# Strassen weights in quarter layout, fifth and sixth product exchanged, chores of the first mixer tied to landed exchanges

## The chip, the core and the metric

The kernel runs on one core of a Trainium2 chip. Its time is the device time of one execution in microseconds (us). The kernel before took 1366.08 us (median of 3 runs, 1362.96 to 1366.48).

A core has five engines that run side by side, each with its own stream of instructions in a fixed order: TensorE (PE) multiplies matrices into PSUM banks, VectorE (DVE) and ScalarE (ACT) work on tiles, GpSimd (POOL) does a few products and issues some of the DMAs, SyncE (SP) issues most of the DMAs. An engine waits at an instruction until the semaphores of what it needs are set; all behind it on that engine waits too.

## The reference

Two layers over 512 tokens of width 1024. Layer 0 mixes tokens by eight heads of bidirectional retention and eight heads of 8 x 16 neighbourhood attention, layer 1 by a Mamba-2 scan. Behind each mixer stands a GeGLU channel mixer ("ffn") of width 2816 with a width-3 convolution in front of the activation.

```python
u = rms_norm(x, g) @ w_up                 # 1024 -> 2 x 2816, gate and value
u = depthwise_conv_centered(u, cw, cb)    # width 3 along the tokens
h = gelu(u[..., :2816]) * u[..., 2816:]
x = x + rms_norm(h @ w_down, g_post)
```

In layer 0 the queries and keys of the retention heads are turned by rotary angles first: every head's two halves change places, one is multiplied by the sine, the other by the cosine.

## The kernel before

**A product in three.** Everything is float32, and every matrix is split into a rounded high part and the rest, so that one product becomes three passes: high by high, low by high, high by low (`mm3`, L124 to L126). A weight tile of 128x1024 (512 KB) is loaded by SP into a staging buffer (`wst`, three of them), cast by ACT to its high part (L115), and DVE subtracts that to give the low part (L116). Both parts go to one of four places of `ring`, from where PE takes them.

**Stages.** In the trace the first mixer lies at about 60 to 250 us, its ffn at 270 to 600, the second mixer at 600 to 1015, the second ffn at 1015 to the end.

**The up projection of the ffn.** Of its 22 blocks of 128 gate and 128 value features, twelve are done in six pairs per ffn (`UP` = 6, 8, 10, 14, 16, 18) by Strassen's scheme: seven products instead of eight (`up_strassen`). A pair's weights are a 2x2 matrix of quarters: gate or value, first or second 512 inputs, each for two blocks of features. Each product has 24 matmuls of 256 columns. The weights of the products are, in order: q11 (the A11 product); q12 + q22 (S3); that plus q11, in the tile `gain` (S2); that plus q21 (A22); q11 with a fourth quarter added to it by an accumulating DMA from POOL (L473; R1); q21 (A12); q22 (S4). In memory a quarter lies as two runs of 2 KB in each partition's row of two blocks, and is gathered by an access pattern (`places`).

The products accumulate in three PSUM banks: A11, S2, R1, S4 in bank a (`mm`), S3 and A22 in bank b (`pu`), A12 in bank d (`pu`). Between two products of one bank ACT or DVE reads the intermediate result from it (L497, L500 by ACT; L458 by DVE), and the next product of that bank waits for that reading.

**Order.** A scheduler puts the instructions of every engine in order by the code's order, by priority (`high_priority(60)` draws a step ahead) and by when operands should be ready. The order is fixed when the kernel is built.

**Chores.** While all this runs, POOL prepares the down projection: `sums` (L284) makes 704 KB copies and accumulations of quarters of `w_down` in DRAM. A chore is tied behind the last matmul issued so far (`E.product`). One is issued at each `c` of the strings `PAIRS` in the first mixer, which say in which order the steps of each pair of heads go; in a Strassen pair one is issued behind the second and one behind the fifth product.

**Rotary exchange.** In the first mixer, for queries and for keys of a pair of heads, ACT copies the projected tile to `ra` (L734), four SP DMAs fetch its 32-row bands exchanged into `rb` (L736), POOL multiplies `rb` by the sine (L737), DVE multiplies `ra` by the cosine (L738) and adds the two (L739), and ACT casts the sum to `rq` or `rk` (L720, L722).

**Neighbourhood attention.** The exponentials `e` are scaled by DVE (L856), transposed by PE to `pt` (L864), copied to `w` by ACT or DVE in turn (L866, in `nb_weights`), and multiplied with the values into `y` (L874).

Of the kernel before, what the change touches and what calls it, by code (L numbers as in the profile page):

```python
# [8 lines left out]
F32 = mybir.dt.float32  # L9
# [4 lines left out]
ALU = mybir.AluOpType  # L14
# [3 lines left out]
P = 128  # L18
# [5 lines left out]
FFN = 2816  # L24
# [7 lines left out]
class Env:  # L32
# [33 lines left out]

        self.xh, self.xl = (self.res.tile([P, KD, S], R32, name=n, tag=n) for n in ("xh", "xl"))

    def chore(self, n=1):

        for _ in range(min(n, len(self.chores))):
            self.together([self.chores.pop(0)()], [self.product])

    def wload(self, src, behind=None):

# [319 lines left out]
UP = (6, 8, 10, 14, 16, 18)  # L395
# [41 lines left out]
def up_strassen(E, pool, w_up, f, X, G, V, held):  # L437

    nc, tc = E.nc, E.tc
    low, high = slice(0, HW), slice(HW, S)

    def places(st, s, h):
        return (st.rearrange("p (f c) -> p f c", f=2),
                w_up[s, f:f + 2, :, h * 512:h * 512 + 512].rearrange("f p c -> p f c"))

    def load(pool, name, s, h, tag=None):
        st = pool.tile([P, 1024], F32, name=name, tag=tag or name)
        nc.sync.dma_start(*places(st, s, h))  # L450
        return st

    def parts(st, i):
        hi, lo = E.weight(SKEW if i else 0)
        E.split(hi, lo, st)
        return hi, lo

    add = lambda o, x, y: nc.vector.tensor_tensor(o, x, y, op=ALU.add)  # L458
    q = {}

    def weights(i):
        with tc.high_priority(60):
            if i == 0:
                q[11] = load(E.wst, "wst", 0, 0)
                return parts(q[11], i)
            if i == 1:
                q[12], q[22] = load(E.wst, "wst", 1, 0), load(pool, "wu", 1, 1, f"e{UP.index(f) % 2}")
                add(q[12], q[12], q[22])
                return parts(q[12], i)
            if i == 2:  # L470
                q[0] = E.gain.tile([P, D], F32, name="gain")
                add(q[0], q[11], q[12])
                nc.gpsimd.dma_start(*places(q[11], 1, 0), accum_op=ALU.add, max_dma_last_dim=4096)  # L473
                return parts(q[0], i)
            if i == 3:
                q[21] = load(E.gain, "gain", 0, 1)
                add(q[0], q[0], q[21])
                return parts(q[0], i)
            return parts(q[{4: 11, 5: 21, 6: 22}[i]], i)

    a = E.mm.tile([P, S], F32, name="mm")
    b, d = (E.px.tile([P, S], F32, name="pu", tag="px") for _ in range(2))
    order = ("A11", a), ("S3", b), ("S2", a), ("A22", b), ("R1", a), ("A12", d), ("S4", a)
    for i, (n, bank) in enumerate(order):
        hi, lo = weights(i)
        more = i in (2, 3, 4, 6)
        r = bank.rearrange("p (j c) -> p j c", j=2)
        for j in range(2):
            for k in range(4):
                c = slice(j * 512 + k * P, j * 512 + k * P + P)  # L490
                E.mm3(r[:, j], hi[:, c], lo[:, c], X[n][0][:, k], X[n][1][:, k], not more and j + k == 0, k == 3, more or j > 0)
        if i in (3, 5):
            o = G[:, :, low if i == 3 else high]
            add(o, r, o)
        elif i == 4:
            t = E.tmp.tile([P, 2, HW], F32, name="w5", tag="tmp")
            nc.scalar.copy(t, r)  # L497
            add(V[:, :, low], t, V[:, :, low])
        else:
            nc.scalar.copy({0: G[:, :, high], 1: V[:, :, low], 2: G[:, :, low], 6: V[:, :, high]}[i], r)  # L500
        if i in (1, 4):
            E.chore()
        if i in (3, 5) and held:
            held.pop(0)()


# [79 lines left out]
def log1p_exp_neg(E, alloc, z):  # L586
# [25 lines left out]


PAIRS = (
# [4 lines left out]
)  # L619


def mixer0(E, w0, w_v, w_fm, tabs, dist_d, logit, gn, bias, w_out, g_post_row, done):
# [3 lines left out]
    nc, tc = E.nc, E.tc  # L626
    with ExitStack() as ctx:
        pool = lambda name, bufs: ctx.enter_context(tc.tile_pool(name=name, bufs=bufs))
        one, two, sd, bp = pool("m0", 1), pool("m0b", 2), pool("m0s", 7), pool("m0n", 2)

        rot = one.tile([P, 2, S], F32, name="rot")
# [30 lines left out]
        for s in range(2):  # L662
            ps = [E.mm.tile([P, 512], F32, name="mm") for _ in range(NT)]
            for u in range(4):
                w = w0.pop(0) if w0 else E.wunit(w_v[s, u])
                for t in range(NT):
                    tt = slice(t * P, (t + 1) * P)
                    for i in range(2):
                        k = 2 * u + i
# [56 lines left out]
        def project(p, o, nm):  # L726
            i = ("rk", "rq", "rg", "nq", "nk").index(nm)
            w = E.wunit(w_fm[i, p])
            ps = E.mm.tile([P, S], F32, name="mm")
            E.proj_fm(ps, w)  # L730
            if i < 2:
                a = E.tmp.tile([P, S], F32, name="ra", tag="tmp")
                b = E.tmp.tile([P, S], F32, name="rb", tag="tmp")
                nc.scalar.activation(a, ps, AF.Copy, scale=1.0 if i else 0.125)  # L734
                for j in range(4):
                    nc.sync.dma_start(b[32 * j:32 * j + 32], a[32 * (j ^ 1):32 * (j ^ 1) + 32])  # L736
                nc.gpsimd.tensor_tensor(b, b, rot[:, 1], op=ALU.mult)  # L737
                nc.vector.tensor_tensor(a, a, rot[:, 0], op=ALU.mult)  # L738
                nc.vector.tensor_tensor(a, a, b, op=ALU.add)  # L739
                o[nm] = (twice if i else stack)(nm, a)  # L740
                o[nm + "a"] = a
            elif i == 2:
                o[nm] = two.tile([P, S], F32, name=nm)
                nc.scalar.activation(o[nm], ps, AF.Silu)
            elif i == 3:
                o[nm] = stack(nm, ps.rearrange("p (r b c) -> p b r c", r=8, b=4))
            else:
                o[nm] = twice(nm, ps, 0.125)
# [110 lines left out]
        def nb_weights(p, o, i):  # L859

            pt = E.px.tile([P, 2, 2, P], F32, name="pt", tag="px")
            for j in range(2):
                for k in range(2):
                    nc.tensor.transpose(pt[:, j, k], o["e", i][:, j, k * P:(k + 1) * P], E.ident)  # L864
            o["w", i] = sd.tile([P, 2, 2, P], F32, name="w", tag="sd")
            (nc.scalar.copy if i % 2 else nc.vector.tensor_copy)(o["w", i], pt)  # L866

        def nb_values(p, o):
            y = E.px.tile([P, 4, P], F32, name="y", tag="px")
# [487 lines left out]
def _cols(w):  # L1357

    f = w.shape[1]
    return w.reshape(KD, P, f // P, P).transpose(2, 1, 0, 3).reshape(f // P, P, 1024)  # L1360
# [42 lines left out]
def _layouts(np, i):  # L1403
    a = {"x": i["x"][0]}
# [32 lines left out]

    for l in range(2):
        w = i["ffn_w_up"][l]
        a[f"f{l}_up"] = np.stack([_cols(w[:, s * FFN:(s + 1) * FFN]) for s in range(2)])  # L1440
        cw = np.concatenate([i["ffn_conv_w"][l], i["ffn_conv_b"][l][None]])
        a[f"f{l}_cw"] = cw.reshape(4, 2, NF, P).transpose(3, 1, 2, 0)
        a[f"f{l}_down"] = _quarters(np, i["ffn_w_down"][l])
# [29 lines left out]
```

## Time and profile before

| | |
|---|---|
| median of 3 runs | 1366.08 us (1362.96 to 1366.48) |
| profiled execution | 1359.76 us, its span 1358.0 us |
| granted clock of TensorE, mean | 0.999 |
| PE busy | 1328.2 us (98% of the span) |
| DVE busy | 1106.3 us (81%) |
| ACT busy | 829.8 us (61%) |
| POOL busy | 127.4 us (9%) |
| bytes moved | 236.23 MB, of it 52.43 MB by POOL's queue |

The page of the profile comes from one execution. Its span runs from the first instruction to the last; 1.76 us of the execution lie around it. PE counts as busy from the start of a matmul to its modelled end, so that matmuls that overlap in the pipeline hide small waits: what PE waits for is better read from the list of waits, or from the starts of its matmuls.

### The profile page before, as it was taken

The page shows a single profiled execution, that of the slowest core. Times are in us where ns is not written, and L with a number is a line of the kernel's source. Part 1 is how long each engine was busy: PE and PEld are TensorE (multiplying, and loading weights), DVE is VectorE, ACT ScalarE, POOL GpSimd, SP SyncE. Part 2 cuts the span into 40 slices and gives each one's busy share as a digit, 9 for nine tenths or more (in the row PEclk, how much of TensorE's full clock was granted, in tenths as well). Part 3 has the DMA queues.
Part 4 walks back from the last instruction along what each step waited for, and adds up shares of the span by engine and source line. Part 5 has one row for each costly group of instructions (what it writes and reads, how often), then busy time and mean ns, then how long its engine had stood idle before and what let it go on. Part 6 is the DMA issues. An engine that isn't in the chain of part 4 may idle for free.

```text
span 1358.0 us, 20142 instructions
## 1 busy us (share of the span) xinstructions
PE 1328.2 (98%) x7640; PEld 1134.6 (84%) x7640; DVE 1106.3 (81%) x1536; ACT 829.8 (61%) x1337; POOL 127.4 (9%) x142
## 2 busy tenths in 40 slices
PE   7999999999999999999999999999999999999997
PEld 6877877898999988888778788787879899998886
DVE  7368778696699998797878876798789789989886
ACT  5356667453564666564878878477545467566663
POOL 1011111111110000010000110011011111110001
PEclk9999999999999999999999999999999999999999
DMA  8454446339894545663565475285545788884554
GB/s 300 143 185 152 159 154 211 105 120 225 177 211 116 143 132 189 198 203 130 139 183 190 129 250 184 92 246 165 183 132 180 191 196 192 192 201 140 190 181 148
DMA packets 78785, 236.23 MB, mean 174 GB/s; under 512 B 8544, under 2 KB 9312, under 8 KB 78176
## 3 DMA queue, kind: packets, MB, share of 16 engines
q1 hardware_dynamic: 60368, 167.30, 37.5%
q0 software_dynamic: 10432, 52.43, 17.1%
q10 hardware_dynamic: 7888, 15.21, 4.2%
q8 instruction: 60, 0.98, 0.3%
q14 instruction: 37, 0.30, 0.1%
HBM read 227.30 MB, written 51.64 MB: 205 GB/s over the span
## 4 chain that ended last, share of the span: by engine, by line
PE 72%; DVE 9%; DMA 7%; ACT 6%; issue 4%; POOL 1%; SPq 0%; DVEq 0%; POOLq 0%; ACTq 0%
PE mm L124 19%; PE mm L126 19%; PE mm L125 19%; DMA pb<-pd 2%; DVE ring L116 2%; PE pu L125 2%; DMA wst<-in_f_up 2%; PE pu L126 2%; PE pu L124 2%; ACT pb L1115 1%; PE st L1085 1%; PE pi L1136 1%; DMA rb<-ra 1%; ACT ring L115 1%; PE pt L181 1%
## 5 line engine op out<-in xcount | busy, mean ns | idle before, releaser
L124 PE MATMUL mm<-xh,ring 128*128 128x512 f32 (+2 forms) x928 | 341.4, 368 | 1.0 <-ACT z L1055 0.4
L126 PE MATMUL mm<-xl,ring 128*128 128x512 f32 (+2 forms) x928 | 340.6, 368 | 1.1 <-DVE mean L939 0.6
L125 PE MATMUL mm<-xh,ring 128*128 128x512 f32 (+2 forms) x928 | 340.3, 367 | 1.0 <-DVE ring L116 1.0
L116 DVE TENSOR_TENSOR ring<-wst,ring 128x1024 fp32r<-128x1024 f32 (+1 forms) x220 | 266.9, 1219 | 64.8 <-ACT ring L115 64.5
L115 ACT CAST ring<-wst 128x1024 fp32r<-128x1024 f32 (+1 forms) x220 | 226.2, 1034 | 123.8 <-PE mm L125 62.4
L124 PEld LDWEIGHTS mm<-xh,ring 128*128 128x128 f32 (+1 forms) x928 | 174.4, 188 | 31.2 <-issue 2.6
L126 PEld LDWEIGHTS mm<-xl,ring 128*128 128x128 f32 (+1 forms) x928 | 174.1, 188 | 30.7 <-issue 1.3
L125 PEld LDWEIGHTS mm<-xh,ring 128*128 128x128 f32 (+1 forms) x928 | 174.4, 188 | 29.2 <-DVE ring L116 1.4
L1115 ACT ACTIVATE pb<-pb,tok 128x128 f32<-128x128 f32 x256 | 80.7, 393 | 11.5 <-DMA pb<-pd 10.3
L124 PE MATMUL mm<-xc,ring 128*128 128x256 f32 x288 | 80.1, 278 | 1.7 <-ACT G L500 1.7
L125 PE MATMUL mm<-xc,ring 128*128 128x256 f32 x288 | 79.9, 277 | 0.0
L126 PE MATMUL mm<-xc,ring 128*128 128x256 f32 x288 | 79.8, 277 | 0.0
L124 PE MATMUL mm<-ring,big 128*128 128x512 f32 x164 | 64.0, 390 | 0.0
L126 PE MATMUL mm<-ring,big 128*128 128x512 f32 x164 | 63.8, 389 | 0.0
L125 PE MATMUL mm<-ring,big 128*128 128x512 f32 x164 | 63.8, 389 | 0.0
L518 ACT ACTIVATE cv<-mm,cwt 128x512 f32<-128x512 f32 x40 | 31.1, 777 | 52.1 <-PE mm L126 52.1
L284 POOL DMA_DIRECT2D ts<-in_f_down x48 | 32.0, 674 | 285.5 <-PE mm L126 206.1
L124 PEld LDWEIGHTS mm<-xc,ring 128*128 128x128 f32 x288 | 54.1, 188 | 2.1 <-ACT G L500 2.1
L126 PEld LDWEIGHTS mm<-xc,ring 128*128 128x128 f32 x288 | 54.1, 188 | 0.0
L125 PEld LDWEIGHTS mm<-xc,ring 128*128 128x128 f32 x288 | 54.0, 188 | 0.0
L125 PE MATMUL pu<-xh,ring 128*128 128x256 f32 x192 | 53.5, 279 | 0.2 <-DVE ring L116 0.2
L124 PE MATMUL pu<-xh,ring 128*128 128x256 f32 x192 | 53.3, 277 | 0.0
(360 smaller groups left out, 3064.2 us busy)
## 6 DMA issues: line engine op xcount, KB each, us to landing
ts<-in_f_down POOLq DMA_DIRECT2D x48, 704.0 KB, 6.2
wst<-in_f_up SPq DMA_DIRECT2D x64, 512.0 KB
wst<-in_c_fm SPq DMA_DIRECT2D x40, 512.0 KB
wst<-ts SPq DMA_DIRECT2D x32, 512.0 KB
pb<-pd ACTq DMA_DIRECT2D x29, 512.0 KB
wst<-in_f_down SPq DMA_DIRECT2D x24, 512.0 KB
ts<-ts POOLq DMA_DIRECT2D x16, 704.0 KB, 8.8
wst<-in_ab_fm SPq DMA_DIRECT2D x20, 512.0 KB
```

The source lines that it names most:

```text
L115: first = self.nc.scalar.copy(hi, src)
L116: second = self.nc.vector.tensor_tensor(lo, src, hi.bitcast(F32), op=ALU.subtract)
L124: mm(out, lh, rh, start=first, stop=False)
L125: mm(out, ll, rh, start=False, stop=False)
L126: self.product = mm(out, lh, rl, start=False, stop=last)
L181: last = nc.tensor.transpose(pt[:, j], xs[:, j * P:(j + 1) * P], self.ident)
L284: out.append(lambda i=i, src=src, j=j, c=c, kw=kw: gp.dma_start(part(ts, i, c), part(src, j, c), **kw))
L518: nc.scalar.activation(o, ps, AF.Identity, scale=w(1), bias=w(3))
L1085: nc.tensor.matmul(ps, o["bt"][:, c], xs, start=True, stop=True)
L1115: nc.scalar.activation(pb[:, dr, c], pb[:, dr, c], AF.Identity, scale=1.0 - 2 * dr, bias=tok[:, 0, c, dr * H + h:dr * H + h + 1])
L1136: nc.tensor.matmul(pi[:, c - 1 + dr], o["st"][dr, i][:, q * P:(q + 1) * P], o["t"][1][:, c * C:(c + 1) * C], start=True, stop=True)
```

## The change

1. The host lays the weights of the twelve Strassen blocks out by quarters, and a quarter's load is one contiguous run of 4 KB per partition instead of two of 2 KB. This holds for the three loads on SP per pair, for the fourth into `gain`, and for POOL's accumulating DMA.
2. The products go in the order 0, 1, 2, 3, 5, 4, 6: A12 comes before R1. The second chore stays behind the fifth product, which is now A12; the two places at which a pending tail of the blocks before is issued stay behind the fourth and the sixth.
3. The staging buffer of q12 is allocated ahead of that of q11.
4. In the first mixer the chore behind a pair's `v2` (in the strings: `v2 c`) is left out, and one is issued behind POOL's sine multiplication of the pair's second exchange instead, tied to that multiplication.
5. The copies to `w` in `nb_weights` get priority 60.

```diff
-    def chore(self, n=1):
+    def chore(self, n=1, behind=None):
...
-            self.together([self.chores.pop(0)()], [self.product])
+            self.together([self.chores.pop(0)()], [behind or self.product])
...
-    def places(st, s, h):
-        return (st.rearrange("p (f c) -> p f c", f=2),
-                w_up[s, f:f + 2, :, h * 512:h * 512 + 512].rearrange("f p c -> p f c"))
-
-    def load(pool, name, s, h, tag=None):
-        st = pool.tile([P, 1024], F32, name=name, tag=tag or name)
-        nc.sync.dma_start(*places(st, s, h))
+    def load(pool, name, s, h, tag=None, st=None):
+        st = pool.tile([P, 1024], F32, name=name, tag=tag or name) if st is None else st
+        nc.sync.dma_start(st, w_up[s, f + h])
...
             if i == 0:
+                q[12] = E.wst.tile([P, 1024], F32, name="wst")
                 q[11] = load(E.wst, "wst", 0, 0)
...
-                q[12], q[22] = load(E.wst, "wst", 1, 0), load(pool, "wu", 1, 1, f"e{UP.index(f) % 2}")
+                load(E.wst, "wst", 1, 0, st=q[12])
+                q[22] = load(pool, "wu", 1, 1, f"e{UP.index(f) % 2}")
...
-                nc.gpsimd.dma_start(*places(q[11], 1, 0), accum_op=ALU.add, max_dma_last_dim=4096)
+                nc.gpsimd.dma_start(q[11], w_up[1, f], accum_op=ALU.add, max_dma_last_dim=4096)
...
-    for i, (n, bank) in enumerate(order):
+    for i in (0, 1, 2, 3, 5, 4, 6):
+        n, bank = order[i]
...
-        if i in (1, 4):
+        if i in (1, 5):
             E.chore()
-        if i in (3, 5) and held:
+        if i in (3, 4) and held:
...
-    "nq rq rk nk rg c k d s0 m a0 a1 v0 c w0 s2 a2 a3 v2 c w1 w2 n w3 o",
+    "nq rq rk nk rg c k d s0 m a0 a1 v0 c w0 s2 a2 a3 v2 w1 w2 n w3 o",
...
-                nc.gpsimd.tensor_tensor(b, b, rot[:, 1], op=ALU.mult)
+                turned = nc.gpsimd.tensor_tensor(b, b, rot[:, 1], op=ALU.mult)
+                if "ra" in o:
+                    E.chore(behind=turned)
+                o["ra"] = a
...
-            (nc.scalar.copy if i % 2 else nc.vector.tensor_copy)(o["w", i], pt)
+            with tc.high_priority(60):
+                (nc.scalar.copy if i % 2 else nc.vector.tensor_copy)(o["w", i], pt)
```

The scheduler turns this into other orders on the engines. Three places follow, each as the order stands before and as it stands now. Lines of the changed kernel are one to three higher or a few lower than those of the kernel before.

DVE, between the second pair and the third of the first triple of the first ffn. Here `gain_3380` holds the summed weights of the second pair's A22 product, `wst_3578` before and `wst_3549` after are the third pair's q12, `gain_3611` its S2 weights, `wst_3318` before and `wst_3319` after the second pair's q11 (for R1), `gain_3410` the second pair's q21 (for A12). A row in which `ring` comes from a weight tile makes the low part. Before:

```order
L458 TENSOR_TENSOR gain_3380<-gain_3380,gain_3410 128x1024
L520 SCALAR_TENSOR_TENSOR cv0_3440<-G_3102,cwt_2558,cv0_3440 128x511
L519 SCALAR_TENSOR_TENSOR cv1_3445<-V_3103,cwn_2560,cv1_3445 128x511
L116 TENSOR_TENSOR ring_69<-gain_3380,ring_69 128x1024
L520 SCALAR_TENSOR_TENSOR cv1_3445<-V_3103,cwn_2560,cv1_3445 128x511
L458 TENSOR_TENSOR wst_3578<-wst_3578,wu_3580 128x1024
L116 TENSOR_TENSOR ring_69<-wst_3318,ring_69 128x1024
```

And now:

```order
L454 TENSOR_TENSOR gain_3380<-gain_3380,gain_3410 128x1024
L519 SCALAR_TENSOR_TENSOR cv0_3440<-G_3102,cwt_2558,cv0_3440 128x511
L518 SCALAR_TENSOR_TENSOR cv1_3445<-V_3103,cwn_2560,cv1_3445 128x511
L454 TENSOR_TENSOR wst_3549<-wst_3549,wu_3580 128x1024
L116 TENSOR_TENSOR ring_69<-gain_3380,ring_69 128x1024
L116 TENSOR_TENSOR ring_69<-gain_3410,ring_69 128x1024
L519 SCALAR_TENSOR_TENSOR cv1_3445<-V_3103,cwn_2560,cv1_3445 128x511
L454 TENSOR_TENSOR gain_3611<-wst_3550,wst_3549 128x1024
```

The sum for the third pair (`wst` from `wst` and `wu`), which needs a load, has moved ahead of the low part of the second pair's A22 weights.

PE, at the end of the first pair. `mm_3104` is bank a of that pair, `pu_3106` its bank d, `mm_3315` bank a of the second pair; `xc` marks combined operands (here R1, then S4), `xh` and `xl` the plain ones. Before, the end of A12's 24 matmuls, which followed on R1's last, and S4's first:

```order
L124 MATMUL pu_3106<-xh_61,ring_69 128x256
L125 MATMUL pu_3106<-xh_61,ring_69 128x256
L126 MATMUL pu_3106<-xl_62,ring_69 128x256
L124 MATMUL mm_3104<-xc_2878,ring_69 128x256
L125 MATMUL mm_3104<-xc_2878,ring_69 128x256
```

And now, R1's last, six of the next pair's A11, and S4's first:

```order
L126 MATMUL mm_3104<-xc_2878,ring_69 128x256
L124 MATMUL mm_3315<-xh_61,ring_69 128x256
L125 MATMUL mm_3315<-xh_61,ring_69 128x256
L126 MATMUL mm_3315<-xl_62,ring_69 128x256
L124 MATMUL mm_3315<-xh_61,ring_69 128x256
L125 MATMUL mm_3315<-xh_61,ring_69 128x256
L126 MATMUL mm_3315<-xl_62,ring_69 128x256
L124 MATMUL mm_3104<-xc_2878,ring_69 128x256
```

Between R1 and S4, which share bank a, there were 24 matmuls and there are 6 now. This is so behind the first two pairs of each triple; behind the third the scheduler puts four matmuls of 512 columns of a plain block between them.

ACT, in the first mixer between the first and the second pair of heads. `rq0` and `rq1` are the turned queries, `w_938` the copy of transposed exponentials, `rs` and `cat4` belong to the normalisation and the output. Before:

```order
L820 ACTIVATE sq_923<-y_839 128x512
L720 ACTIVATE rq0_997<-ra_987 64x512
L722 ACTIVATE rq0_997<-ra_987 64x512
L866 COPY w_938<-pt_933 128x512
L825 ACT_TABLE_LOAD
L825 ACTIVATE rs_927<-rs_927 128x512
```

And now:

```order
L822 ACTIVATE sq_923<-y_840 128x512
L719 ACTIVATE rq0_997<-ra_987 64x512
L869 COPY w_938<-pt_933 128x512
L827 ACT_TABLE_LOAD
L827 ACTIVATE rs_927<-rs_927 128x512
L879 COPY cat4_553<-y_940 128x4x8x16
L721 ACTIVATE rq0_997<-ra_987 64x512
```

The copy to `w_938` still stands behind the first cast of the turned queries, but the second cast has moved behind it and behind the normalisation.

More of the change, by code (lines that the diff above doesn't have):

```diff
@@ L1439, in _layouts @@
         w = i["ffn_w_up"][l]
-        a[f"f{l}_up"] = np.stack([_cols(w[:, s * FFN:(s + 1) * FFN]) for s in range(2)])
+        w = np.stack([_cols(w[:, s * FFN:(s + 1) * FFN]) for s in range(2)])
+        for f in UP:
+            w[:, f:f + 2] = w[:, f:f + 2].reshape(2, 2, P, 2, 512).transpose(0, 3, 2, 1, 4).reshape(2, 2, P, 1024)
+        a[f"f{l}_up"] = w
         cw = np.concatenate([i["ffn_conv_w"][l], i["ffn_conv_b"][l][None]])
```

6 rows, old and new, of the table PAIRS are left out of this document.

## The prediction, as it was put on record

> **What bounds the kernel now.** I read the page first, then the waits of PE by stage, then the timeline around the longest of them. The page gives the span, how busy each engine is, and the shares of the chain that ended last:
>
> ```profile
> span 1358.0 us, 20142 instructions
> PE 1328.2 (98%) x7640; PEld 1134.6 (84%) x7640; DVE 1106.3 (81%) x1536; ACT 829.8 (61%) x1337; POOL 127.4 (9%) x142
> PE 72%; DVE 9%; DMA 7%; ACT 6%; issue 4%; POOL 1%; SPq 0%; DVEq 0%; POOLq 0%; ACTq 0%
> ```
>
> PE is busy nearly throughout, and the change takes no matmul away. So it can gain only what PE waits for at the places that it touches. Those waits in the first mixer (60 to 250 us):
>
> ```profile
> PE y L874 <- ACT w L866: 2.8, 2, 1.5
> PE sc L795 <- DVE rk L700: 0.9, 1, 0.9
> ...
> PE pt L864 <- DVE e L856: 0.5, 1, 0.5
> PE y L874 <- DVE w L866: 0.2, 1, 0.2
> ```
>
> and in the first ffn's Strassen pairs (320 to 500 us), then the second's (1080 to 1230):
>
> ```profile
> PE mm L124 <- ACT G L500: 1.7, 2, 1.3
> ```
>
> ```profile
> PE pu L125 <- DVE ring L116: 0.2, 1, 0.2
> ```
>
> The columns are total us, times, longest. What the change speaks to in the mixer is L874 and L864, 2.8 + 0.5 + 0.2 = 3.5 us; in the ffns 1.7 + 0.2 = 1.9 us. Together 5.4 us, 0.4% of the time, is the cap on the listed gain.
>
> **Part 1: chores behind landed exchanges.** The timeline at the second exchange of the first pair of heads:
>
> ```profile
> 100.48 2.42 SPq L736 DMA_DIRECT2D rb<-ra  x4
> 102.28 0.49 POOL L284 DMA_DIRECT2D ts<-in_f_down  x1 [8.31 <-PE y L812]
> ...
> 105.39 0.61 DVE L856 TENSOR_SCALAR e<-e,sm 128x256 f32<-128x256 f32 x2
> ...
> 107.36 1.77 POOL L737 TENSOR_TENSOR rb<-rb,rot 128x512 f32<-128x512 f32 x1 [4.59 <-DMA rb<-ra]
> 107.92 1.62 DVE L856 TENSOR_SCALAR e<-e,sm 128x256 f32<-128x256 f32 x2
> ...
> 110.83 0.63 ACT L720 ACTIVATE rq<-ra 64x512 fp32r<-64x512 f32 x1 [3.78 <-DVE ra L739]
> ...
> 112.14 0.59 ACT L866 COPY w<-pt 128x512 f32<-128x512 f32 x1
> 112.77 1.09 PE L874 MATMUL y<-w,nvt 128*64 128x128 f32 x14 [1.28 <-ACT w L866]
> ```
>
> The chore's 704 KB go out while the exchange's four transfers are issued; the exchange lands 6.88 us after its first issue (100.48 to POOL's start at 107.36). ACT then stands at `rq`, idle for 3.78 us, with the copy to `w` queued behind it, and PE waits 1.28 us for that copy. The same at the third pair:
>
> ```profile
> 186.10 4.81 SPq L736 DMA_DIRECT2D rb<-ra  x4
> ...
> 186.72 0.49 POOL L284 DMA_DIRECT2D ts<-in_f_down  x1 [8.39 <-PE y L812]
> ...
> 192.48 1.78 POOL L737 TENSOR_TENSOR rb<-rb,rot 128x512 f32<-128x512 f32 x1 [5.27 <-DMA rb<-ra]
> ...
> 195.01 0.63 ACT L720 ACTIVATE rq<-ra 64x512 fp32r<-64x512 f32 x1 [3.98 <-DVE ra L739]
> 195.55 0.56 ACT L866 COPY w<-pt 128x512 f32<-128x512 f32 x1
> ...
> 196.16 1.09 PE L874 MATMUL y<-w,nvt 128*64 128x128 f32 x14 [1.52 <-ACT w L866]
> ```
>
> Here it takes 6.38 us. An exchange without a chore beside it:
>
> ```profile
> 116.99 2.41 SPq L736 DMA_DIRECT2D rb<-ra  x4
> ...
> 120.95 1.30 POOL L737 TENSOR_TENSOR rb<-rb,rot 128x512 f32<-128x512 f32 x1 [1.03 <-DMA rb<-ra]
> ```
>
> takes 3.96 us. With the chore issued behind the multiplication, the exchange should come 6.88 - 3.96 = 2.9 and 6.38 - 3.96 = 2.4 us sooner, both more than PE's waits of 1.28 and 1.52. At the first place the second `rq` cast also leaves the way of `w`, another 0.63 us. So the 2.8 us go. The 0.5 us before the transposes go with `e`: two scalings took 1.62 us while POOL's multiplication ran (107.36 to 109.13), against 0.61 for two at 105.39. A multiplication that starts 2.9 us sooner, at 104.5, lies beside that other pair or another DVE step and may slow it as much. I leave the 0.5 in and count 2.8 + 0.2 = 3.0 us gained; 3.5 is the upper bound, and 2.8 - 1.0 = 1.8 the lower, if those 1.62 - 0.61 = 1.0 us fall on a step that PE waits for.
>
> The Trainium skill ("SBUF — State Buffer", "Who interferes with whom") has it that VectorE's second port pair is GpSimd's too and is locked, not shared, by an instruction; the 1.62 us agree. By that rule the lock only moves with the multiplication, and the lower bound would hold if it met a step that is waited for.
>
> What it moves: four chores start some 5 us later, after the multiplication. They then run beside the loads of weights that follow. POOL has 9% of its time busy and no instruction between waits for a chore's issue (0.49 us), so POOL costs nothing. The down projection's quarters are needed only hundreds of us later.
>
> **Part 2: quarter layout.** Two rows of the chain that ended last show the loads that the ffn's waits hang on (issue at, us to landing), and the timeline what hung on them:
>
> ```profile
> 336.35 8.22 DMA wst<-in_f_up
> ...
> 361.82 11.08 DMA wst<-in_f_up
> ```
>
> ```profile
> 344.64 1.22 DVE L458 TENSOR_TENSOR wst<-wst,wu 128x1024 f32<-128x1024 f32 x1 [4.80 <-DMA wst<-in_f_up]
> ...
> 349.90 0.58 ACT L500 COPY G<-mm 128x512 f32<-128x512 f32 x1
> ...
> 350.54 0.38 PE L124 MATMUL mm<-xc,ring 128*128 128x256 f32 x1 [1.26 <-ACT G L500]
> ...
> 367.07 1.22 DVE L116 TENSOR_TENSOR ring<-gain,ring 128x1024 fp32r<-128x1024 f32 x1
> ...
> 372.57 0.28 PE L124 MATMUL pu<-xh,ring 128*128 128x256 f32 x1
> ...
> 372.93 1.23 DVE L458 TENSOR_TENSOR wst<-wst,wu 128x1024 f32<-128x1024 f32 x1 [3.98 <-DMA wst<-in_f_up]
> ```
>
> DVE stood idle 4.80 us for the second pair's q12 at 344.64; behind it the sum for S2, its cast, and only then the copy G that PE waited 1.26 us for. The loads are slow because POOL's chore shares the sixteen DMA engines with them. The queues in 366 to 369 us (packets, MB, share of the engines' time), and in 358 to 360 us, where only loads ran:
>
> ```profile
> q0 software_dynamic: 123, 0.48, 82.0%
> q1 hardware_dynamic: 105, 0.22, 21.4%
> ```
>
> ```profile
> q1 hardware_dynamic: 321, 0.63, 86.7%
> ```
>
> The two queues move about as many packets each: 123 and 105. A chore's packet (4 KB, accumulating) takes 0.820 x 16 x 3 / 123 = 0.32 us of an engine, a load's 2 KB packet 0.214 x 48 / 105 = 0.098 us (alone 0.867 x 32 / 321 = 0.086). If the engines take the queues' packets in turn, a 512 KB load of 16 packets of 2 KB per engine needs 16 x (0.32 + 0.098) = 6.7 us; as 8 packets of 4 KB it needs 8 x (0.32 + 0.196) = 4.1 us. That is 2.6 us sooner for a load fully beside a chore, and somewhat less, say 1.8, for the one at 336.35, which was beside one in part. Either is above 1.26, so the 1.7 us of waits for G go; with the 0.2 of the second ffn 1.9 us. The bounds are 0 (the turns are not by packet) and 1.9.
>
> **Part 3: the weight sum ahead of the A22 low part.** The order on DVE puts the third pair's sum, at 372.93 before, ahead of the low part of A22's weights, which was made at 367.07, with the product's start at 372.57. With the load 2.6 us sooner the sum runs at 370.3, the low part at 371.55 to 372.77; the second matmul, which needs it, is due at 372.57 + 0.11 = 372.68. So 0.1 us, which I count as 0. With the load at the old time it would be 374.15 + 1.22 = 375.4, 2.7 us late: the second rival.
>
> **Part 4: R1 next to S4.** R1's accumulated weights get a product more time, which no listed wait asks for: counted at nothing. But S4 now waits for ACT's copy of R1 out of the same bank. Before, A12's 24 matmuls covered it:
>
> ```profile
> 358.69 0.28 PE L126 MATMUL mm<-xc,ring 128*128 128x256 f32 x1
> 359.00 0.59 ACT L497 COPY w<-mm 128x512 f32<-128x512 f32 x1 [1.66 <-PE mm L126]
> 359.03 0.28 PE L126 MATMUL pu<-xl,ring 128*128 128x256 f32 x1
> ```
>
> and the ACT side of L497, all twelve:
>
> ```profile
> ACT w L497 <- PE mm L126: 20.4, 12, 1.8
> ```
>
> From the last R1 matmul's start to ACT's is 0.31 us, the copy 0.59, and from ACT's end to PE's start 0.06 (349.90 + 0.58 to 350.54): S4 can start 0.96 us behind. Matmuls start 0.113 us apart (358.69 to 359.03 for three), so six of the next pair put S4's start at 7 x 0.113 = 0.79: it waits 0.17 us, at eight of the twelve pairs 1.3 us. At the four others stand four matmuls of 512 columns, at twice the 0.113: 0.11 + 0.91 = 1.02, no wait. So 1.3 us lost, between 0 and, if nothing covered, 12 x 0.85 = 10 us. I take 1.3, since ACT was idle before all twelve (20.4 / 12 = 1.7 us on average).
>
> **Parts without a price.** The staging buffers come out in the same turns as before when the addresses are laid side by side, so the earlier allocation of q12 changes nothing. The copies to `w` that are drawn ahead on DVE pass one or two scalings of `e`; their wait of 0.2 is in the sum.
>
> **The sum.** -3.0 - 1.9 + 1.3 = -3.6 us on the profiled execution's 1359.76 us (span 1358.0, 1.76 around it), so 1356.2. That execution was faster than all three timed runs; the difference carries over to their median: 1366.08 - 3.6 = 1362.5.
>
> **The rivals.** *All of it, and S4 covered* (chance 0.2): the cap, -5.4, and S4 at 0; with the wait of 0.9 at L795, which hangs on the same DVE queue, -6.3: 1360.7 to 1359.8. For it speaks ACT's idle time ahead of R1's copies.
>
> *Layout brings nothing* (0.15): loads land when they did, so part 2 gives 0 and the moved sum holds A22 for 2.7 us: -3.0 + 1.3 + 2.7 = +1.0, 1367.1; 1365.8 if S4 is covered, 1368.5 if the other three triples lose half of the 2.7 between them. For it speaks that 2 KB packets alone came at 0.086 us each, 16 engines x 2 KB / 0.086 = 380 GB/s, a good rate; against it the nearly equal packet counts of two queues with unequal packets. The Trainium skill ("DMA: Bandwidth & Descriptors", "Specifications") gives 512 B as the smallest transfer for line rate; by that rule 2 KB and 4 KB would be alike and the time 1367.1. It speaks of a transfer by itself, and no row of this profile has two queues with equal packets.
>
> *Hidden anyway* (0.15): the mixer's waits come back at the next step that waits for DVE, which is near full there, as L795 for `rk` does now; only the ffn's -1.9 + 1.3 = -0.6 is left: 1365.5.
>
> *Slower: S4 behind R1's copy* (0.1): if ACT is late, because a cast or a convolution of a tail stands before the copy, or the next pair's A11 weights are not ready when the scheduler's six matmuls should cover it, each of twelve pairs loses 0.85 to 1.3 us: 10 to 15 us, less the gains, 1372 to 1378. It decides from the point at which ACT starts the copy more than 0.5 us late; the 1.7 us of idle time on average speak against it.
>
> **How the numbers follow.** A measurement of this kernel can tell about 0.3% from no change, 4.1 us: faster is below 1362.0, slower above 1370.2. The forecast has 0.40, all of it 0.2, layout nothing 0.15, hidden 0.15, S4 0.1. The timed runs differ by 3.5 us, so a median may be off by some 2. The forecast lies 0.5 us above the bound and gives half its chance to faster, 0.20; all of it gives 0.18, the two middle rivals 0.02: 0.40. Slower has S4's 0.1 and 0.02 of the layout's: 0.12. The rest, 0.48, is the same. The range reaches from all of it less that scatter, 1359.8 - 1.8 = 1358.0, to the upper end of the layout's case, 1368.5; out of it are S4's 0.1 and the tails.
>
> **What would show it.** Right: exchanges of 4 us at all eight places, no wait of L874 for ACT's `w`; `wst<-in_f_up` beside a chore near 8 us instead of 11.08; DVE's sum of the third pair before 371; gaps of about 0.17 us ahead of S4 and none larger. Wrong: waits of PE for `ring` at A22 of 2 us or more (layout), waits for `w` at L497 near a microsecond (S4), or the mixer's stage as long as before with other names in its list.

## The result and the profile after

The changed kernel takes 1361.16 us (median of 20 runs, 1356.89 to 1364.02), the kernel before 1364.09 in the same comparison (20 runs, 1359.76 to 1367.37). The ratio is 0.9976 with a 95% interval of 0.9966 to 0.9986, which is 1.9 to 4.6 us less, 3.3 in the middle. The forecast was 3.6 us less. By the bound of 0.3% it is no change that a single measurement of this kernel could tell; twenty runs on each side do tell it.

The profiled execution's time fell from 1359.76 to 1357.45 us, its span from 1358.0 to 1355.7. The page's lines that answer to those of before:

```profile
span 1355.7 us, 20129 instructions
...
PE 1329.5 (98%) x7640; PEld 1134.4 (84%) x7640; DVE 1108.7 (82%) x1536; ACT 830.3 (61%) x1337; POOL 123.0 (9%) x142
...
PE 85%; DVE 5%; ACT 3%; DMA 3%; issue 2%; POOL 1%; DVEq 0%; SPq 0%; POOLq 0%; ACTq 0%
```

The chain that ended last passes through PE for 85% of the span instead of 72%, and through DMAs for 3% instead of 7%. What PE waits for in the changed kernel, in the first mixer (60 to 250 us):

```profile
PE sc L797 <- DVE rk L699: 1.0, 1, 1.0
PE pt L866 <- DVE e L858: 0.9, 2, 0.5
PE mm L124 <- ACT xh L115: 0.7, 1, 0.7
PE S L783 <- DVE kt L776: 0.4, 1, 0.4
PE y L877 <- ACT w L869: 0.3, 1, 0.3
```

The 2.8 us for ACT's `w` are down to 0.3; the wait for `e` rose from 0.5 to 0.9. In the Strassen pairs (the first fence is 320 to 500 us, the second 1080 to 1230):

```profile
PE mm L124 <- ACT G L499: 0.7, 1, 0.7
```

```profile
PE pu L125 <- DVE ring L116: 0.4, 1, 0.4
```

The wait for G fell from 1.7 to 0.7 us and did not go. The 0.4 us is not the 0.2 of before, which stood at 1174 us and went, but a new wait at 1111 us. A better ruler than these lists is the length of each stage, from the start of PE's transposes (L181) that open it to the start of the next stage's, and for the second ffn to the end of PE's last matmul; it holds small waits too. In us, for every profiled execution, those of the experiments below among them:

| profiled execution | first mixer | first ffn | second mixer | second ffn |
|---|---|---|---|---|
| before | 250.3 | 339.5 | 409.9 | 344.0 |
| before_again | 250.7 | 339.3 | 416.8 | 344.2 |
| before_third | 250.8 | 338.9 | 411.3 | 343.9 |
| changed kernel | 247.4 | 339.4 | 409.1 | 345.4 |
| mix | 247.3 | 347.2 | 411.2 | 344.9 |
| mix_again | 247.2 | 341.5 | 410.2 | 343.1 |
| mix_chores | 247.7 | 339.7 | 410.2 | 344.2 |
| lay | 250.5 | 337.1 | 411.1 | 344.7 |
| swap_only | 251.1 | 341.3 | 411.7 | 346.9 |
| noswap | 248.7 | 336.8 | 413.4 | 344.8 |
| halves | 248.8 | 339.9 | 412.9 | 342.6 |
| halves_again | 248.7 | 336.8 | 411.2 | 342.6 |
| no_acc | 248.1 | 337.4 | 411.4 | 344.4 |
| no_chore5 | 247.5 | 338.2 | 410.6 | 345.8 |

Against the three executions of before, the changed kernel's first mixer is 2.9 to 3.4 us shorter, its first ffn 0.1 shorter to 0.5 longer and its second ffn 1.2 to 1.5 longer. The change gave in the first mixer what was forecast; in the ffns it lost more than it won.

What it lost there shows on PE. The timeline of the changed kernel where the last matmul of the first pair's R1 is followed by six of the next pair's A11 (`xh`, `xl`; the last three shown) and then by S4 (`xc`):

```profile
358.67 0.59 ACT L496 COPY w<-mm 128x512 f32<-128x512 f32 x1 [1.78 <-PE mm L126]
...
358.84 0.28 PE L124 MATMUL mm<-xh,ring 128*128 128x256 f32 x1
358.96 0.28 PE L125 MATMUL mm<-xh,ring 128*128 128x256 f32 x1
359.07 0.28 PE L126 MATMUL mm<-xl,ring 128*128 128x256 f32 x1
...
359.31 0.38 PE L124 MATMUL mm<-xc,ring 128*128 128x256 f32 x1
359.54 0.28 PE L125 MATMUL mm<-xc,ring 128*128 128x256 f32 x1
```

ACT's copy ends at 359.26 and S4 starts at 359.31, 0.24 us behind the matmul before instead of 0.113: a wait of 0.13. The next start is 0.23 us on, another 0.11 lost. This pair of delays stands at eight places of the trace, four in each ffn.

### The profile page after: what moved, and what is told of

Its sections match the earlier page's. It is cut to its first block, busy times and chain, and to the rows that moved or that the text cites. A ratio compares the mean times of both kernels' runs of the same rounds, so it can differ in the third digit from the quotient of the medians.

```text
span 1355.7 us, 20129 instructions
## 1 busy us (share of the span) xinstructions
PE 1329.5 (98%) x7640; PEld 1134.4 (84%) x7640; DVE 1108.7 (82%) x1536; ACT 830.3 (61%) x1337; POOL 123.0 (9%) x142
## 4 chain that ended last, share of the span: by engine, by line
PE 85%; DVE 5%; ACT 3%; DMA 3%; issue 2%; POOL 1%; DVEq 0%; SPq 0%; POOLq 0%; ACTq 0%
PE mm L124 23%; PE mm L126 22%; PE mm L125 22%; PE pu L125 2%; PE pu L126 2%; PE pu L124 2%; DMA wst<-in_f_up 2%; PE pi L1139 2%; PE st L1088 1%; DVE ring L116 1%; PE py L1159 1%; PE pt L181 1%; PE pd L126 1%; PE pd L125 1%; PE pd L124 1%
## 5 line engine op out<-in xcount | busy, mean ns | idle before, releaser
L124 PE MATMUL mm<-xh,ring 128*128 128x512 f32 (+2 forms) x928 | 341.5, 368 | 0.5 <-ACT xh L115 0.2
```

What stands on the lines that cost most here:

```text
L124: mm(out, lh, rh, start=first, stop=False)
```

## The experiments

Each kernel is timed against the kernel before, run on the same chip. Kernels with a ratio have 6 to 12 runs of their own, the others one.

**mix: the mixer's part alone.** The edit is the change's `chore(..., behind)`, the four strings, `turned` and the priority, and nothing in `up_strassen` or on the host:

```diff
+                turned = nc.gpsimd.tensor_tensor(b, b, rot[:, 1], op=ALU.mult)
+                if "ra" in o:
+                    E.chore(behind=turned)
...
+            with tc.high_priority(60):
```

> The kernel before with the first mixer's part alone: chores behind landed exchanges, and the copies to w at priority. By the sum of pieces the two waits of PE for ACT's w (2.8 us) shrink to 0.3 and the second ffn starts 3.0 us sooner, as in the changed kernel: span 1358.0 - 3.0 = 1355.0, ratio 0.9978; the ffns keep their waits for G (1.7). Rival, hidden anyway: the waits come back in the stage and the ratio is within 0.0005 of 1.

Measured: 1361.79 us against 1364.31, ratio 0.9981 (0.9965 to 0.9997). The first mixer took 247.3 us, 3.0 less than the first profile of before and within 0.1 of the changed kernel's. "Hidden anyway" falls. The span was 1364.9, though, by a wait in the first ffn that no one had forecast (320 to 500 us):

```profile
PE mm L124 <- ACT G L500: 8.5, 1, 8.5
```

The timeline shows a load (`wst`, by SP) issued at 337.42, with three of POOL's transfers on the DMA engines before it had landed at 348.9 (POOL, and DVE's sum behind the load):

```profile
334.86 1.25 POOL L473 DMA_DIRECT2D wst<-in_f_up  x1 [14.69 <-DVE ring L116]
335.65 1.46 POOL L284 DMA_DIRECT2D ts<-ts  x1
341.08 0.86 POOL L284 DMA_DIRECT2D ts<-ts  x1 [3.98 <-PE mm L126]
```

```profile
348.92 1.23 DVE L458 TENSOR_TENSOR wst<-wst,wu 128x1024 f32<-128x1024 f32 x1 [10.27 <-issue]
```

A chore waits for a matmul, a load for a free buffer. In the kernel before the second chore came at 344.09, when its load had all but landed (DVE's sum at 344.64); here it came at 341.08 and lay over the load. The load was late to begin with: an earlier load had held DVE for 6.58 us, up to a sum at 327.10, where in the second execution of this kernel it was 2.41 us, up to 322.94.

**mix_again: was that chance?** The same kernel.

> The mixer part alone once more. Its first profiled execution had one wait of 8.7 us for G in the first ffn (347.2 us instead of 339.5), since three of POOL's transfers lay over one load. If that belongs to the order of this kernel, it is here again, 5 us or more. If it is chance, the first ffn takes 339 to 341 us and the span is about 1355 plus what the second mixer takes above 410.

Measured: 1358.07 us, first ffn 341.5, one wait for G of 2.0 us. So the 8.5 us were not the order's alone. The first ffn is longer than before's in both executions all the same (347.2 and 341.5 against 338.9 to 339.5). In the second, 1.7 of these us are the clock's: behind the wait PE ran 3.4 us at half clock. In these rows of a stretch of the trace each, the granted clock is the third number from the right:

```profile
346.00:349.00 3.00, 0.95 (x8) 0.76 (x7) 2.96 (x4) 2.26 (x3) 0.85 (x1) 1.00 0.52 72
349.00:352.40 3.40, 3.40 (x18) 3.40 (x17) 3.40 (x5) 1.65 (x3) 0.00 (x0) 0.50 0.96 192
352.40:356.00 3.60, 3.60 (x33) 3.60 (x32) 2.31 (x3) 1.73 (x3) 0.00 (x0) 1.00 0.61 170
```

**mix_chores: without the priority.** As mix, without `tc.high_priority(60)`.

> The mixer part alone without the priority of the copies to w: only the chores are moved behind landed exchanges. If the exchange's late landing made the waits of PE for w (2.8 us), they are gone or below 0.5 and the first mixer takes about 247.5 us, as with both. If the order of ACT (second cast of the turned queries ahead of w) made them, half of them or more stay and the first mixer takes 249 or more.

Measured: 1357.78 us, first mixer 247.7, and in its list of waits for 60 to 250 us:

```profile
PE y L877 <- ACT w L869: 0.3, 1, 0.3
```

The waits for `w` go by the chores alone: ACT's order there is that of before, with both casts of the turned queries ahead of the copy. The priority is worth 0.5 us at most (247.7 against 247.2 and 247.3).

**lay: the quarter layout alone**, in the kernel (shown) and on the host.

```diff
-        nc.sync.dma_start(*places(st, s, h))
+        nc.sync.dma_start(st, w_up[s, f + h])
...
-                nc.gpsimd.dma_start(*places(q[11], 1, 0), accum_op=ALU.add, max_dma_last_dim=4096)
+                nc.gpsimd.dma_start(q[11], w_up[1, f], accum_op=ALU.add, max_dma_last_dim=4096)
```

> The kernel before with the quarter layout alone; every engine's order is that of before. If the two queues take turns by packets, as the prediction had it, the load beside a chore lands 2.6 us sooner (11.08 to about 8.5) and the waits for G (1.7) go: about -1.9 us. If the load is held by something that the layout does not shorten, it lands 0.6 to 1.5 us sooner, as in the changed kernel, and a part of the wait for G stays (1.26 to about 0.7): -0.6 to -1.3 us. If the layout brings nothing: 0.

Measured: 1359.96 us against 1364.31, ratio 0.9963 (0.9947 to 0.9980), 2.7 to 7.2 us less. Its waits in the first ffn, then in the second:

```profile
PE mm L124 <- ACT G L496: 0.5, 1, 0.5
```

```profile
PE pu L125 <- DVE ring L116: 0.8, 1, 0.8
```

The two loads beside transfers of POOL land in 7.6 us (336.63 to DVE's sum at 344.18) and 9.4 (361.68 to 371.05), where before had 8.3 and 11.1: 0.7 and 1.7 us sooner. That is the second case of the expectation. The first ffn is 1.8 to 2.4 us shorter, the second 0.5 to 0.8 longer: its wait of 0.8 us stands at the place where before's three profiles have 0.2, 0.3 and 0.6. The timed gain is larger than these stages account for; see the end of the next section.

**swap_only: the exchange of products alone**, with the second chore and the pending tail moved as in the change.

```diff
-    for i, (n, bank) in enumerate(order):
+    for i in (0, 1, 2, 3, 5, 4, 6):
+        n, bank = order[i]
```

> The kernel before with fifth and sixth product exchanged, without layout. By the sum of pieces it is slower: eight waits of 0.13 us and eight slow restarts of 0.11 ahead of S4 (+1.9), and the weight sum that stands ahead of A22's low part waits for the old loads, about 2.7 us late at the first triple and less at the others (+3 to +5): ratio 1.0035 to 1.005. Rival, that the exchange itself earns something, by the more time for R1's weights: ratio 1.000 or below.

Measured: 1368.31 us against 1364.31, ratio 1.0026 (1.0009 to 1.0042), slower. Its waits, first ffn and second:

```profile
PE mm L124 <- ACT G L501: 1.5, 1, 1.5
PE pu L125 <- DVE ring L116: 0.9, 1, 0.9
```

```profile
PE pu L125 <- DVE ring L116: 1.7, 1, 1.7
```

The wait for G stays, two waits for A22's low part (`pu`, `ring`) come in, and the pair of delays ahead of S4 stands at eight places again. The first ffn is 1.8 to 2.4 us longer than before's, the second 2.7 to 3.0. The direction is as expected, the size less: 1.2 to 5.7 us timed, where the sum of the pieces was 4.9 to 6.9.

**noswap: the change without the exchange.** As the changed kernel, with `enumerate(order)`, and the chore and the tail where they stood.

> The changed kernel with the products in the old order; mixer part, layout and earlier allocation stay. By the sum of pieces it loses nothing ahead of S4 (1.9) nor at A22 (0.4 + 0.7) and keeps -3.0 and the layout's -0.6 to -1.9: -3.6 to -4.9 us, ratio 0.9964 to 0.9974, some 2 to 3 us below the changed kernel's trace (1355.7). Rival, that the exchange earns something: at or above the changed kernel, ratio 0.9976 or more, span 1355.7 or more.

Measured: 1357.70 us against 1364.31, ratio 0.9938 (0.9918 to 0.9959), below the interval of the changed kernel (0.9966 to 0.9986). "The exchange earns something" falls. The first ffn is 336.8 us, 2.6 below the changed kernel's; the profile has no delay ahead of S4. Its first mixer's extra 1.3 us lie ahead of everything that is changed: PE's first matmuls of 512 columns start 0.43 us apart until 15.8 us, where those of the changed kernel are 0.23 apart from 13.6 us on. Both executions of the next kernel begin in the same way.

**halves: A12 cut in two.** A12's first twelve matmuls go ahead of R1, its other twelve between R1 and S4:

```diff
-        for j in range(2):
+        def half(j, n=n, hi=hi, lo=lo, r=r, more=more):
...
+        half(0)
+        if i == 5:
+            second = half
+            continue
+        half(1)
+        if i == 4:
+            second(1)
...
-        if i in (1, 5):
+        if i in (1, 4):
             E.chore()
```

> The changed kernel with A12's product cut in two: twelve matmuls ahead of R1, twelve behind it. If S4's price is the wait for ACT's copy and the slow restart, 8 x (0.13 + 0.11) = 1.9 us, it is gone, since twelve matmuls of 0.113 cover the 0.96 us: ratio about 0.14% below the changed kernel's, 0.996 against before, and no wait ahead of S4 in the trace. Rival, that the exchange's price lies only in the order of DVE, where the third pair's weight sum stands ahead of A22's low part: the ratio stays at 0.9976 and the waits ahead of A22 with it.

Measured: 1355.33 us against 1364.47, ratio 0.9934 (0.9914 to 0.9954). Nothing is left ahead of S4: its start follows 0.12 us on the matmul before (`pu` is A12, `mm` from `xc` is S4):

```profile
362.42 0.28 PE L126 MATMUL pu<-xl,ring 128*128 128x256 f32 x1
362.54 0.28 PE L124 MATMUL mm<-xc,ring 128*128 128x256 f32 x1
```

Neither ffn has a wait at A22 either, and the second takes 342.6 us, the shortest of all. The edit also issues the second chore behind R1 and the whole of A12, so what was won at A22 and at the loads is not shown to be the cut's alone.

**halves_again.** The same kernel, since its first profiled execution was the longest of its six.

> The version with A12 cut in two a second time; its first profiled execution (1358.1 us) was the longest of its six runs. Stages then: first mixer 248.8, first ffn 339.9, second mixer 412.9, second ffn 342.6. If the scatter of the second mixer and of the load behind the wait for G (2.0 us) made that run long, this one, if it is near the median of 1355.3 us, has the second mixer at 409 to 411 and the wait for G below 1; the second ffn stays at 342 to 343, 3 us below the changed kernel's 345.4.

Measured: 1354.90 us; 248.7, 336.8, 411.2 and 342.6. What differed from the first time was mostly the first ffn (339.9), with a wait for G of 0.2 us instead of 1.8 and without the 3.4 us at half clock that had followed that one. The two second ffns agree to the tenth.

**no_acc and no_chore5: what the load waits behind.** The changed kernel without one of POOL's two transfers:

```diff
-                nc.gpsimd.dma_start(q[11], w_up[1, f], accum_op=ALU.add, max_dma_last_dim=4096)
```

> The changed kernel without POOL's accumulating DMA into q11 (the R1 product takes q11 alone, so the fourth quarter is left out); every other engine's order is the same. If that transfer holds up the load issued behind it, the second pair's and the third's q12 land 5 to 6 us after their issue instead of 7.6 and 9.6, and the waits for G (0.7) and ahead of A22's low part (0.4 and 0.7 with the restarts) go. If the chore behind it holds the load, they land within 1 us of 7.6 and 9.6.

```diff
-        if i in (1, 5):
+        if i == 1:
             E.chore()
+        elif i == 5 and E.chores:
+            E.chores.pop(0)
```

> The changed kernel without the chore behind the fifth product (twelve of the copies and sums of the down projection's quarters are left out, so the down projection uses what is there); every other engine's order is the same. If the chore is what the load shares the engines with, as the prediction had it, the third pair's q12 lands 5 to 6 us after its issue instead of 9.6. If the accumulating DMA ahead of it holds the load, the load lands some 2 us behind that DMA's landing, 7 us or more after its issue.

Measured: 1356.79 and 1358.22 us, spans 1355.0 and 1356.5. DVE's sum behind the third pair's q12 in the changed kernel, without the accumulation, and without the chore:

```profile
367.81 1.23 DVE L454 TENSOR_TENSOR wst<-wst,wu 128x1024 f32<-128x1024 f32 x1 [3.15 <-DMA wst<-in_f_up]
```

```profile
363.87 1.22 DVE L454 TENSOR_TENSOR wst<-wst,wu 128x1024 f32<-128x1024 f32 x1
```

```profile
364.16 1.22 DVE L454 TENSOR_TENSOR wst<-wst,wu 128x1024 f32<-128x1024 f32 x1
```

The loads were issued at 358.18, 357.57 and 357.76. DVE did not wait for the last two, so they took at most 6.3 and 6.4 us, against 9.6. Leaving out either transfer is enough; how long each alone holds the load is not shown, since 6.3 and 6.4 are upper bounds. The second pair's load, which lies behind an accumulation and a chore of a plain block, lands in 4.4 us without the accumulation (334.11 to 338.50), and in 7.2 in no_chore5, which leaves both in that place (333.54 to 340.74). The list of PE's waits is empty for 320 to 500 and 1080 to 1230 us without the accumulation. So neither case of the expectations held as it was put, that one of the two would prove to be the cause: it is both together, one behind the other in POOL's queue.

**before_again and before_third: the scatter.** The kernel before, unchanged.

> The kernel before, unchanged, once more, for a second profiled execution. The profile shown of it (1359.76 us) is the fastest of its executions, whose median is some 4 us higher. If the ffn's loads beside POOL's transfers make that scatter, this execution, if it is longer, has the mixers' stages within 0.5 us of the first profile and its extra time in waits of PE for ACT's G or DVE's ring in the Strassen pairs (3.6 us in the first ffn or the second). Rival, the scatter is spread over all stages or comes from the clock: every stage is longer by the same share.

> The kernel before a third time, for its stages. In two executions its first mixer and both ffns agreed within 0.4 us (250.3 and 250.7; 339.5 and 339.3; 344.0 and 344.1) and the second mixer took 409.9 and 416.8. If the scatter is the second mixer's, those three stages come out within 0.5 us of that again and the second mixer between 409 and 417. Rival: an ffn has a stall of its own in some executions, as the one of 8.7 us in the mixer part alone: then an ffn is longer by 3 us or more.

Measured: 1367.11 and 1360.82 us. The second mixer took 416.8 and 411.3 us against 409.9; the other stages agree within 0.6. So the expectation that the Strassen pairs make the scatter fell at the first, and that of the second held. The longest waits of the second mixer (600 to 1010 us) in before_again:

```profile
PE mm L124 <- ACT z L1055: 2.9, 1, 2.9
PE mm L124 <- DVE xf L1049: 2.7, 2, 2.0
```

and in the first profile of before:

```profile
PE mm L124 <- DVE xf L1049: 1.1, 2, 0.7
...
PE mm L124 <- ACT z L1055: 0.4, 1, 0.4
```

The clock adds to these waits. The wait for `z` ends at 693.80, the longer one for `xf` at 836.17, and around them PE's clock was half for 6.8 and 3.4 us, which makes up to 5.1 of the 6.9 us between 409.9 and 416.8:

```profile
693.00:700.00 7.00, 6.20 (x15) 4.90 (x16) 2.95 (x5) 6.97 (x18) 0.00 (x0) 0.52 0.53 140
836.30:839.70 3.40, 3.40 (x9) 2.64 (x10) 0.00 (x0) 3.39 (x6) 0.00 (x0) 0.50 0.15 58
```

## Why the prediction came out right, and where it was wrong

The time came out 1.3 us below the forecast's 1362.5, and that close it is by luck. The forecast started from a median of 1366.08 us of three runs; in the comparison the kernel before has 1364.09, 2.0 less, from which -3.6 gives 1360.5. The change itself, -2.9 us between the medians, is near the forecast, but the terms as measured do not add up to it: one was right, and the three others all came out worse than forecast.

**Part 1, the chores: -3.0 forecast, -2.9 to -3.4 measured.** The mechanism and the size held, and mix_chores shows the cause. The two exchanges that had taken 6.88 and 6.38 us take 3.99 and 3.98 from first issue to multiplication:

```profile
100.59 2.43 SPq L735 DMA_DIRECT2D rb<-ra  x4
...
104.58 1.31 POOL L736 TENSOR_TENSOR rb<-rb,rot 128x512 f32<-128x512 f32 x1 [10.55 <-DMA rb<-ra]
```

```profile
184.33 2.42 SPq L735 DMA_DIRECT2D rb<-ra  x4
...
188.31 1.28 POOL L736 TENSOR_TENSOR rb<-rb,rot 128x512 f32<-128x512 f32 x1 [11.79 <-DMA rb<-ra]
```

The forecast's sign was 4 us at all eight exchanges: six have it, the three of 6.09 to 6.88 among them; the first (5.5) and the sixth (5.0) are as before. The wait for `e`, counted as staying at 0.5, rose to 0.9. POOL's multiplication now runs from 104.58 to 105.89, and DVE's step at 104.94 takes 1.37 us where the same step 0.81 us earlier takes 0.61:

```profile
104.13 0.61 DVE L759 SCALAR_TENSOR_TENSOR toep<-dist,lg,toep 128x384 f32<-128x384 f32 x1
...
104.94 1.37 DVE L759 SCALAR_TENSOR_TENSOR toep<-dist,lg,toep 128x384 f32<-128x384 f32 x1
106.23 0.60 DVE L858 TENSOR_SCALAR e<-e,sm 128x256 f32<-128x256 f32 x2
106.72 0.63 PE L866 MATMUL pt<-head,e 128*128 128x128 f32 x4 [0.53 <-DVE e L858]
```

The scalings of `e` behind it take their usual 0.60, and PE waits 0.53 us for them. The rule of the Trainium skill that the prediction named ("SBUF — State Buffer", "Who interferes with whom") is borne out: the lock moved with the multiplication, onto a step with two inputs from SBUF ahead of the one that PE waits for.

**Part 2, the layout: -1.9 forecast.** The loads came 0.6 us sooner (8.22 to 7.62, the second pair) and 1.5 (11.08 to 9.61, the third), where 1.8 and 2.6 were forecast. The waits for G went from 1.7 to 0.7 and the 0.2 of the second ffn went: -1.2 instead of -1.9. The step that failed is "if the engines take the queues' packets in turn" over the whole load. It was read off 366 to 369 us, the load's last part. Earlier, between 363 and 365 us of before, with the load issued at 361.82, the software queue has every packet and the load's queue none:

```profile
q0 software_dynamic: 156, 0.31, 88.6%
```

That is the accumulation of R1's weights, which landed at 367.03. Beside the chore the turns are as forecast: from 364 to 367 us of the changed kernel the two queues moved 92 and 97 packets. The prediction named only the chore; the runs without the one or the other show that both count. The Trainium skill ("DMA: Bandwidth & Descriptors", "Queues, rings and completion order") has an engine drain a whole packet of several descriptors from one queue before it turns to the next; the 156 to 0 agree with turns longer than one packet of the trace, and no run here shows where a turn ends.

**Part 3, the weight sum: 0 forecast, 1.1 measured.** The load landed 1.1 us later than the forecast's 2.6 allowed for, so the sum ahead of A22's low part held PE up by 0.29 us at the first triple and by 0.60 at the second ffn's, each with 0.11 more at the next matmul. The direction was the second rival's, the size less than half of its 2.7.

**Part 4, S4: 1.3 forecast, 1.9 measured.** The wait was forecast at 0.17 us and is 0.13. What the term left out is the restart: the second matmul after each of these waits starts 0.11 us late. 8 x (0.13 + 0.11) = 1.9. The four other pairs' four matmuls of 512 columns cover the copy but for 0.01 us, and there the second matmul starts 0.02 late.

**The sum.** By these terms -3.2 - 1.2 + 1.1 + 1.9 = -1.4 us; the span fell by 2.3, and 0.8 of the rest lies in the second mixer, which the change doesn't touch (409.9 to 409.1) and which scatters by more. Of the four rivals none came as such: the second had the direction of part 3, the slower one the place of part 4, and its point of decision, ACT more than 0.5 us late at R1's copy, was not reached.

**What stays open.** The timed gains of the kernels with the new layout are larger than their stages say: lay -5.0 us timed against -2.1 + 0.7 = -1.4 in the two ffns; halves -9.0 against -2.5 and -5.8 in its two profiles, without the second mixer. The exchange (+5.0 in two stages, +1.2 to +5.7 timed) and the mixer's part agree better. The second mixer does not explain it: its seven profiles without the layout average 411.6 us, its seven with it 411.4.

The granted clock explains a part of it for lay and halves. Of the 36 timed executions of before that the experiments on two chips were compared with, 15 have a mean clock of 0.997 or less, which in the profiles always goes with a stretch at half clock, with a median of 1366.9 us, against 1363.1 of the 21 others. Of lay's eight executions none has it that low, of halves' six one. Among executions of 0.998 or more lay is 3.3 us below before and halves 7.2. But noswap, with three of six that low, comes to 8.8 in the same way, against -4.2 in its three stages. Of the changed kernel's 20 executions one has it that low; for the 20 of before beside them no clock is on record. The rest is not settled, nor why the waits that lower the clock come in some executions and not in others.

## What to carry to other kernels

A copy in DRAM that nobody waits for costs time by the transfers it lies beside: tie it to an instruction behind their landing, and look at each queue for everything that is on the engines in that stretch, not only for the transfer last added. When two products that share a PSUM bank become neighbours, count the matmuls between them against the copy's start, length and hand-over (0.96 us here), and add to every stop 0.11 us for the restart and up to 0.1 for what follows. Look for waits near 2 us that come in some executions only: here one of 2.0 us cost another 1.7 by the clock. Time the parts of a change one by one: the exchange of products was a loss inside a gain, and the changed kernel without it (0.9938), or with A12 cut in two (0.9934), beats both kernels.

## What the runs showed of the hardware

After a wait, PE's second matmul starts 0.11 us late, whether the wait was 0.13 or 1.3 us. And matmuls of 256 columns come at two spacings, 0.113 us and 0.117 to 0.118. At the eight places where S4 stopped, the rest of its 24 matmuls came at the wider one: 2.82 us from the first start to the last, against 2.61 in ten of noswap's twelve; 0.11 of the difference is the restart, 0.1 the spacing. No list of waits holds this. In their two ffns the three profiles of before have 848 to 1032 matmuls at the wider spacing (0.1155 to 0.125 us) and the changed kernel 989, but noswap has 730 and halves_again 612, which is 0.5 to 1.3 and 1.0 to 1.8 us of what these gain. What ends a stretch of it is not shown.

After the wait of 8.5 us in mix PE ran at half clock for 4 us; stretches before, in, behind it and after that (the granted clock is the third number from the right):

```profile
340.00:346.00 6.00, 6.00 (x51) 5.88 (x50) 0.00 (x0) 0.00 (x0) 0.86 (x1) 1.00 1.05 231
346.00:354.70 8.70, 0.27 (x3) 0.07 (x1) 5.71 (x7) 2.76 (x5) 0.85 (x1) 0.65 0.79 151
354.80:358.80 4.00, 3.98 (x18) 3.99 (x19) 4.00 (x5) 2.34 (x3) 0.00 (x0) 0.50 0.02 4
358.90:363.00 4.10, 4.10 (x37) 4.10 (x37) 2.51 (x3) 1.93 (x3) 0.00 (x0) 1.00 0.64 190
```

Some 19 matmuls started 0.21 us apart instead of 0.113, so the wait cost about 2 us beyond its length. Between 60 and 1340 us of the fourteen profiles the clock fell at every listed wait of PE of 2.0 us or more (2.0, 2.0, 2.2, 2.9 and 8.5), at two of the four of 1.8 and 1.9, and at no shorter one, each time for 3.4, 6.8 or 10.2 us. In mix it fell at 348.7, 2.4 us after PE had stopped. The Trainium skill ("TensorE: Matmul & The Clock Gate", Part 1: The HAM clock gate) has the clock halved after an idle window of about 3.4 us and restored after a busy one as long. The lengths at half clock agree, as multiples of that window; the idle time does not, since 1.8 to 2.2 us of it were enough here.
